# Two weight chunks share runs of equal matmuls

## The chip, the cores and the metric

The kernel runs on one core of one Trainium2 chip. The metric is the device time of one execution in microseconds (us): 1226.41 us is the median of three runs of the kernel before (1226.11 to 1227.22). The engines are TensorE (PE in the rows; PEld are its weight loads), VectorE (DVE), ScalarE (ACT), GpSimd (POOL) and SyncE (SP), whose queue issues nearly all DMAs.

## The reference, cut to what matters

Two transformer blocks run one after the other on 256 tokens of 1024 features, all in float32. Every projection is a product of activations with a large weight matrix that is read from HBM once.

```
x = x + 0.5 * swiglu(rmsnorm(x), ff1_w_gate, ff1_w_up, ff1_w_down)      # d_ff 2816
h = rmsnorm(x); proj = h @ w_in                                         # gMLP, q, k, v, gates
y_a = gmlp_spatial_gating(...); y_b = stick_breaking_attention(q, k, v)
x = x + (g_a * (y_a @ w_branch_a) + g_b * (y_b @ w_branch_b)) @ w_out
x = rmsnorm(x + 0.5 * swiglu(rmsnorm(x), ff2_w_gate, ff2_w_up, ff2_w_down))
# second block, two layers:
for layer in (moba attention, forgetting attention):
    x = x + attention(...) @ w_o[layer]
    x = x + square(relu(rmsnorm(x) @ w_up[layer])) @ w_down[layer]      # 4096 wide
out = rmsnorm(x)
```

## The kernel before, in words

A float32 product is computed with three fp32r products. Each operand is split in a part hi (rounded to fp32r) and a part lo (the rest), and hi * hi + hi * lo + lo * hi is kept.

Weights stream through in **chunks** of 128 x 1024 numbers (512 KB). For every chunk the sync queue fills one of six `raw` buffers; the Scalar engine copies it to one of five `whi` buffers (line 143, `split_hi`); the Vector engine subtracts to make one of four `wlo` buffers (line 150, `split_lo`), and behind each subtraction the DMA of a further chunk is issued. These copies run ahead in program order: before unit u the kernel places the hi copy of chunk u + 3 and the lo copy of chunk u + 2.

A **group** is a set of output columns, mostly 512, that accumulates over its chunks in four PSUM banks; groups alternate between the rings psA and psB of four banks each. A **unit** is the work of PE on one chunk, or on two at the end of some groups. In a *wide* group (all the feed-forward and down projections and some others) the output is transposed: the weights are the stationary operand, and the activations, hi beside lo, move through. A chunk of a group of 512 columns has 128 x 128 weights eight times (two tiles of the inner dimension by four banks). For each there is one **hi matmul** (whi against 512 columns, activations hi and lo) and one **lo matmul** (wlo against 256 columns, activations hi). Line 161 issues all of them.

What sets the order on PE is `unit_mm`. A unit of a wide group does its eight hi matmuls and then its eight lo ones if it is an even unit of the group, and lo first if it is odd. Two chunks in turn are thus hi, lo, lo, hi, and where a pair meets the next one two hi runs join. All engines run the order that the program writes (`manual_schedule`); nothing is reordered later.

The evacuations of a group are queued around the units that follow it: `pre` before the copies of a unit, `mid` between these copies and PE's work, `at` behind it. In a feed-forward part (`ffn`: 11 groups of 4 chunks, each 256 gate and 256 up columns) the Scalar engine copies the upper halves of two banks (line 355), the Vector engine adds the lower halves (361) and multiplies by the norm's factor (563), a Silu follows (566), then the same for the up banks (361, 576), the product (577) and the split of the hidden tile (541, 538). In a squared-ReLU part (`mlp`: 8 groups of 4 chunks) the chain is lines 355, 361, 1055, 1058, 541, 538, once for each half. The norm's factor is computed while the first group of a part (`lead`) is on PE, so the lead's evacuations wait for it and are queued later than those of other groups. A down projection (`down`) has two groups of 512 columns, of 11, 16 or 4 chunks; the last two chunks of its second group share a unit in which bank after bank is finished (`stagger`). `down` is used for the ends of both `ffn`, for the first `mlp`'s end and for w_out, whose input, the merged branches, the Vector and Scalar engines make just ahead of it (lines 937 to 946).

Of the kernel before, what the change touches and what calls it, by code (L numbers as in the profile page):

```python
# [26 lines left out]
class Group:  # L27
# [3 lines left out]


    def __init__(self, ring, srcs, ktiles, xin, tok=False, stagger=0, wide=False, head=0):
        self.head = head
        self.ring, self.srcs, self.ktiles, self.xin = ring, srcs, ktiles, xin
        self.tok, self.stagger, self.wide = tok, stagger, wide
        self.width = sum(c for _, _, c in srcs)
        self.banks = self.width // (128 if wide else 256)
        self.kph = 1024 // self.width
        self.ps = None  # L40
# [3 lines left out]
def decoder_kernel(  # L44
# [58 lines left out]
    def add(g):  # L103
        g.u0 = len(units)
        hs = []
        for k0 in range(0, g.ktiles, g.kph):
            hs.append(len(halves))
            halves.append((g, k0))
        n = len(hs) - g.stagger
        if g.head:  # L110
            units.append((g, hs[:g.head]))
        units.extend((g, [h]) for h in hs[g.head:n])
        if g.stagger:
            units.append((g, hs[n:]))
        g.u1 = len(units) - 1
        return g
# [36 lines left out]
    def unit_mm(u):  # L153
        g, hs = units[u]
        if g.ps is None:
            g.ps = [bank(g.ring) for _ in range(g.banks)]
            g.started = [False] * g.banks
        seq = [(h, kl) for h in hs for kl in range(g.kph)]

        def mm(b, dst, lhsT, rhs, stop):  # L160
            PE.matmul(dst, lhsT, rhs, start=not g.started[b], stop=stop, skip_group_check=True)  # L161
            g.started[b] = True

        def orders(i):

            return (("hi", "lo") if i % 2 == 0 or u < 4 else ("lo", "hi")) if g.wide else ((0, 1, 2),)

        def ws(h, kl, b, parts=(0, 1, 2), end=True):
            k = halves[h][1] + kl
            last = end and k == g.ktiles - 1  # L170
            if g.wide:
                col = kl * g.width + b * 128
                wh, wl = hi_t[h][:, col:col + 128], lo_t[h][:, col:col + 128]
                x = g.xin(k, b)
                if parts == "hi":
                    mm(b, g.ps[b], wh, both(x), last)
                elif parts == "lo":
                    mm(b, g.ps[b][:, :T], wl, x[:, 0, :], last)
                for i in parts if len(parts) == 1 else ():
                    mm(b, g.ps[b][:, T:] if i == 1 else g.ps[b][:, :T], wl if i == 2 else wh,  # L180
                       x[:, int(i == 1), :], False)
                return
            for j in range(2):
                nt = 2 * b + j
                col = kl * g.width + nt * 128
                wh, wl = hi_t[h][:, col:col + 128], lo_t[h][:, col:col + 128]
                x = g.xin(k, nt)
                dst = g.ps[b][:, j * T:(j + 1) * T]
                for i in parts:
                    mm(b, dst, wl if i == 2 else wh, x[:, int(i == 1), :], last and j == 1 and i == 2)  # L190

        def tsm(h, kl, tok, chs, c=slice(0, 512), d=0):
            k = halves[h][1] + kl
            last = k == g.ktiles - 1
            nch = g.width // 512
            xh, xl = (g.xin(k, 0)[:, i, tok * 128:(tok + 1) * 128] for i in range(2))
            for w in (hi_t[h], lo_t[h]):
                for ch in chs:
                    col = kl * g.width + ch * 512
                    b = tok * nch + ch + d  # L200
                    mm(b, g.ps[b][:, :c.stop - c.start], xh, w[:, col + c.start:col + c.stop], False)
            for ch in chs:
                col = kl * g.width + ch * 512
                b = tok * nch + ch + d
                mm(b, g.ps[b][:, :c.stop - c.start], xl, hi_t[h][:, col + c.start:col + c.stop], last)

        if g.tok:
            nch = g.width // 512
            if len(hs) > 1:
                for b in range(g.banks):  # L210
                    n = 1 if b < g.banks - 1 else 2
                    for i in range(n):
                        if i:
                            g.ps.append(bank(flip(g.ring)))
                            g.started.append(False)
                        for h, kl in seq:
                            tsm(h, kl, b // nch, (b % nch,), slice(i * 512 // n, (i + 1) * 512 // n), i)
            else:
                for h, kl in seq:
                    for tok in range(2):  # L220
                        tsm(h, kl, tok, range(nch))
        elif len(hs) > 1:
            for b in range(g.banks):
                o = orders(u - g.u0 + b)
                for i in o:
                    for h, kl in seq:
                        ws(h, kl, b, i, i == o[-1])
        elif u == 0:
            for b in range(g.banks):
                if b == 2:  # L230
                    x_bank(1)
                for i in range(3):
                    for h, kl in seq:
                        ws(h, kl, b, (i,))
        else:
            o = orders(u - g.u0)
            for i in o:
                if u == 1 and i == o[-1]:
                    x_turn(3)
                for h, kl in seq:  # L240
                    for b in range(g.banks):
                        ws(h, kl, b, i, i == o[-1])
# [301 lines left out]
    def ffn(ring, name, wg, wu, wd, slots):  # L544
        r, lead = ring, None
        for i in range(DFF // 256):
            g = add(Group(r, [(wg, 256 * i, 256), (wu, 256 * i, 256)], 8, hn_in, wide=True))
            if lead is None:
                lead = g
                at(g.u0, hidden(name, slots))  # L550
                norm_at(g.u0, r, own=True)

            def gate2(g=g):
                g.gate = second(g, 0, "gt")

            def early(g=g):
                first(g, 0, g.gate)
                first(g, 1, g.up)

            def gate1(g=g):  # L560
                if g is not lead:
                    first(g, 0, g.gate)
                V.tensor_mul(g.gate, g.gate, bc2(R["bc"]))

            def gate0(g=g):
                S.activation(g.gate, g.gate, AF.Silu)
                if g is not lead:
                    g.up = second(g, 1, "ut")

            def up2(g=g):  # L570
                g.up = second(g, 1, "ut")

            def up1(g=g):
                if g is not lead:
                    first(g, 1, g.up)
                V.tensor_mul(g.up, g.up, bc2(R["bc"]))
                V.tensor_mul(g.up, g.up, g.gate)

            def up0(g=g, i=i):
                put_hidden(g.ev + 2, name, 2 * i, g.up)  # L580

            g.ev = max(g.u1, lead.u0 + 5)
            if g is lead:
                at(g.u0 + 4 - (g.u0 > 0), gate2)
                at(g.u0 + 4, up2)
                pre(g.u0 + 5, early)
            else:
                at(g.ev, gate2)
            pre(g.ev + 1, gate1)
            mid(g.ev + 1, gate0)  # L590
            pre(g.ev + 2, up1)
            mid(g.ev + 2, up0)
            r = flip(r)
        return down(r, wd, DFF // 128, fixed_in(name))

    def down(r, w, ktiles, xin, stagger=2):

        return [add(Group((r, flip(r))[i], [(w, 512 * i, 512)], ktiles, xin, stagger=i * stagger, wide=True))
                for i in range(2)]

    at(10, w_s_prep, B)
    for i in range(3):
# [33 lines left out]
    gates = []  # L636
    for i in range(4):
        gates.append(add(Group(r, [(win, 5120 + i * 512, 512)], 8, hn_in, wide=True)))
        r = flip(r)
    norm_at(gates[0].u0, gates[0].ring, cols=True, own=True)  # L640
    lnp = {}
# [37 lines left out]
    for i in range(2):  # L679
        r = flip(r)  # L680
        gu.append(add(Group(r, [(win, 512 * i, 512)], 8, hn_in, wide=True)))

    def gv_evac(b):
        if b == 0:
# [357 lines left out]
    def mlp(ring, name, w, slots):  # L1042
        r, lead = ring, None
        for i in range(8):
            g = add(Group(r, [(w, 512 * i, 512)], 8, hn_in, wide=True))
            if i == 0:
                at(g.u0, hidden(name, slots))
                norm_at(g.u0, r, own=True)
# [345 lines left out]
```

## Time and profile before

| what | value |
|---|---|
| median of three runs | 1226.41 us (1226.11 to 1227.22) |
| profiled execution | 1225.88 us |
| its span | 1224.1 us |
| PE busy | 1214.8 us, 99% of the span |
| weight loads (PEld) busy | 1086.3 us, 89% |
| DVE busy | 893.0 us, 73% |
| ACT busy | 724.0 us, 59% |
| DMA | 219.56 MB, mean 179 GB/s |
| granted TensorE clock | full in all 40 slices |

The span is the time from the first to the last instruction of the program; the execution's own time is 1.8 us longer. Times in rows are us from the span's start. A matmul's duration in a row overlaps the next matmul, so its pace is read from starts. In a timeline, matmuls of one line, tile and shape that follow each other are one row with their count; a window that begins inside a run shows only the rest of the run. Tile names stand without numbers; `hn` is the normed activation, `ffa`, `ffb` and `ma` hidden tiles, `mg` the merged branches, `gt`, `ut` and `rl` temporaries of the evacuations.

### The profile page before, as it was taken

The numbers are of one execution on the slowest core, as the hardware profiler recorded it, in microseconds if no ns is written. First come the engines' busy times: TensorE is split into PE (matmuls) and PEld (weight loads), VectorE is DVE, ScalarE is ACT, GpSimd is POOL, SyncE is SP. The second block draws the span as 40 slices with busy tenths as digits, with TensorE's granted clock in tenths as the row PEclk, the third lists the DMA queues.
The fourth block names the chain that finished last, engine by engine and source line by source line (L and its number), as shares of the span: only waits on it lengthen the run. The fifth ranks groups of instructions, "written<-read, shape, count | busy, mean of one in ns | idle before, by whom it ended". The sixth has DMA issues, their size and how long they took to land.

```text
span 1224.1 us, 20196 instructions
## 1 busy us (share of the span) xinstructions
PE 1214.8 (99%) x7754; PEld 1086.3 (89%) x7754; DVE 893.0 (73%) x1453; ACT 724.0 (59%) x1193; POOL 1.9 (0%) x7
## 2 busy tenths in 40 slices
PE   9999999999999999999999999999999999999997
PEld 8888888889999988888899899888889899888886
DVE  7977756769657688778679767876557767887644
ACT  7655546754666566555466656765446566776433
POOL 0000000000000000000000000000000000000000
PEclk9999999999999999999999999999999999999999
DMA  8666656655444566665565445656564634465651
GB/s 274 214 193 200 208 189 190 191 188 165 152 149 136 160 188 186 192 191 184 190 195 155 142 139 169 189 190 214 165 215 140 232 123 154 156 206 189 227 196 42
DMA packets 143409, 219.56 MB, mean 179 GB/s; under 512 B 10088, under 2 KB 81360, under 8 KB 143312
## 3 DMA queue, kind: packets, MB, share of 16 engines
q1 hardware_dynamic: 141568, 213.79, 54.6%
q10 hardware_dynamic: 1744, 4.48, 1.1%
q8 instruction: 61, 1.00, 0.3%
q14 instruction: 36, 0.29, 0.1%
HBM read 217.17 MB, written 1.06 MB: 178 GB/s over the span
## 4 chain that ended last, share of the span: by engine, by line
PE 96%; DVE 3%; issue 0%; ACT 0%; DMA 0%; DVEq 0%; ACTq 0%
PE psA L161 52%; PE psB L161 37%; PE psB L846 1%; PE psB L825 1%; DVE wlo L150 1%; PE psA L846 1%; PE psA L825 1%; PE psB L888 0%; PE psB L731 0%; DMA xin<-in_x_dram 0%; DVE gv L721 0%; PE psB L890 0%; DVE gv L717 0%; DVE st L706 0%; PE psA L969 0%
## 5 line engine op out<-in xcount | busy, mean ns | idle before, releaser
L150 DVE TENSOR_TENSOR wlo<-raw,whi 128x1024 fp32r<-128x1024 f32 x403 | 483.9, 1219 | 103.8 <-issue 60.5
L143 ACT ACTIVATE whi<-raw 128x1024 fp32r<-128x1024 f32 x403 | 416.4, 1053 | 136.9 <-PE psA L161 81.0
L161 PE MATMUL psA<-hn,whi 128*128 128x512 f32 (+1 forms) x1224 | 267.3, 345 | 0.2 <-ACT whi L1282 0.2
L161 PEld LDWEIGHTS psA<-hn,whi 128*128 128x128 f32 x1224 | 209.6, 190 | 25.9 <-ACT whi L1282 0.4
L161 PE MATMUL psB<-hn,whi 128*128 128x512 f32 (+1 forms) x832 | 196.7, 375 | 0.0
L161 PEld LDWEIGHTS psB<-hn,whi 128*128 128x128 f32 x832 | 149.2, 189 | 25.2
L161 PE MATMUL psA<-hn,wlo 128*128 128x256 f32 x960 | 165.6, 283 | 0.1
L161 PEld LDWEIGHTS psA<-hn,wlo 128*128 128x128 f32 x960 | 139.7, 191 | 4.2 <-DVE wlo L150 0.5
L161 PE MATMUL psB<-hn,wlo 128*128 128x256 f32 x768 | 109.6, 283 | 0.0
L161 PEld LDWEIGHTS psB<-hn,wlo 128*128 128x128 f32 x768 | 102.6, 191 | 3.6
L161 PE MATMUL psA<-whi,mb 128*128 128x512 f32 (+1 forms) x256 | 69.1, 386 | 0.0
L161 PEld LDWEIGHTS psA<-whi,mb 128*128 128x128 f32 x256 | 47.8, 188 | 9.6
L988 ACT ACTIVATE sc<-sc,mx 128x256 f32<-128x256 f32 x64 | 28.4, 445 | 30.7 <-DVE sm L985 30.7
L161 PE MATMUL psA<-whi,hn 128*128 128x512 f32 x128 | 41.7, 395 | 0.0
L161 PE MATMUL psA<-wlo,mb 128*128 128x512 f32 (+1 forms) x128 | 40.3, 386 | 0.0
L161 PE MATMUL psA<-ma,whi 128*128 128x512 f32 x128 | 30.9, 391 | 0.0
L1058 ACT ACTIVATE rl<-rl 128x512 f32<-128x512 f32 x32 | 20.3, 633 | 17.8 <-DVE rl L1055 17.7
L161 PE MATMUL psB<-ma,whi 128*128 128x512 f32 x128 | 30.7, 391 | 0.0
L161 PEld LDWEIGHTS psA<-whi,hn 128*128 128x128 f32 x128 | 24.0, 188 | 5.2
L161 PEld LDWEIGHTS psA<-wlo,mb 128*128 128x128 f32 x128 | 24.0, 188 | 4.9
L386 DVE SCALAR_TENSOR_TENSOR xT<-rs,xT 128x512 f32<-128x512 f32 x16 | 11.0, 688 | 23.7 <-ACT rs L355 23.6
L161 PEld LDWEIGHTS psB<-ma,whi 128*128 128x128 f32 x128 | 23.5, 188 | 4.6
(318 smaller groups left out, 1834.2 us busy)
## 6 DMA issues: line engine op xcount, KB each, us to landing
raw<-in_w_up_dram SPq DMA_DIRECT2D x64, 512.0 KB, 3.9
raw<-in_w_down_dram SPq DMA_DIRECT2D x64, 512.0 KB, 4.0
raw<-in_ff_w_gate_dram SPq DMA_DIRECT2D x88, 256.0 KB, 3.0
raw<-in_ff_w_down_dram SPq DMA_DIRECT2D x44, 512.0 KB, 3.8
raw<-in_ff_w_up_dram SPq DMA_DIRECT2D x86, 256.0 KB, 5.3
raw<-in_w_in_dram SPq DMA_DIRECT2D x40, 512.0 KB, 4.4
raw<-in_w_in_dram SPq DMA_DIRECT2D x32, 256.0 KB, 2.9
raw<-in_moba_w_qkv_dram SPq DMA_DIRECT2D x32, 256.0 KB, 3.9
```

Source lines behind the costliest of these rows:

```text
L143: S.activation(hi_t[h], raw_t[h].rearrange("p k c -> p (k c)"), AF.Copy)
L150: V.tensor_sub(lo_t[h], raw_t.pop(h).rearrange("p k c -> p (k c)"), raw32(hi_t[h]))
L161: PE.matmul(dst, lhsT, rhs, start=not g.started[b], stop=stop, skip_group_check=True)
L386: V.scalar_tensor_tensor(xb, t, alpha, xb, op0=OP.mult, op1=OP.add)
L825: PE.matmul(hb[t][64 * h:64 * h + 64, 384:512], vv[:, k, c:c + 64], w[:, h * 384 + c0:h * 384 + c0 + 128], start=k == 0, stop=k == t, skip ...
L846: PE.matmul(banks[h][:, c:c + n], left[i][rw, cl:cl + 128], right[j][rw, cr:cr + n], start=start and i + j == 0, stop=i == 1, skip_group_c ...
L988: S.activation(s[:, a:b], s[:, a:b], AF.Exp, bias=mx[:, i:i + 1], accum_out=sm[:, i:i + 1])
L1058: S.activation(t, t, AF.Square)
```

## The change

Groups get a flag `pairs`. It is set in all groups of `down`, and in the groups of `ffn` and `mlp` from the third on. In such a group, units are taken two by two, as long as both are single chunks. The first unit of a pair does one kind of matmul for both chunks c and d, the second the other kind, with the chunks in reverse. Even pairs of a group are hi c, hi d, lo d, lo c; odd pairs are lo c, lo d, hi d, hi c. The number of matmuls, the copies and their places in the other engines' queues, the buffers and the units where evacuations are queued stay as they are. A chunk that has no partner and the staggered units keep the old order.

```diff
-            o = orders(u - g.u0)
+            i = u - g.u0
+            singles = g.u1 - g.u0 + (len(units[g.u1][1]) == 1)
+            if g.pairs and i < singles - singles % 2:
+
+                a = u - i % 2
+                hs2 = [units[a][1][0], units[a + 1][1][0]]
+                o = orders(i // 2)
+                for h in hs2 if i % 2 == 0 else hs2[::-1]:
+                    for kl in range(g.kph):
+                        for b in range(g.banks):
+                            ws(h, kl, b, o[i % 2], i % 2 == 1 and h == hs2[1])
+                return
+            o = orders(i)
...
# in ffn and in mlp:
+            g.pairs = i > 1
...
# in down:
+        for g in gs:
+            g.pairs = True
```

The flag is off in groups that the diff doesn't name. There are 96 pairs, 46 of them odd. In PE's whole order a lo matmul of 256 columns is followed by a hi matmul of 512 in 143 places before and in 96 now; the other way round it is 136 and 90.

The first place is PE in the third group of the first feed-forward part (psA; it is the first one with the flag) and the group after it (psB). In the order before:

```order
L161 MATMUL psA<-hn,whi 128x512 x8
L161 MATMUL psA<-hn,wlo 128x256 x16
L161 MATMUL psA<-hn,whi 128x512 x16
L161 MATMUL psA<-hn,wlo 128x256 x8
L329 MATMUL psB<-ident,w_s 128x128 x4
L1341 MATMUL psB<-ident,gains 128x128
L161 MATMUL psA<-hn,wlo 128x256 x8
L161 MATMUL psA<-hn,whi 128x512 x8
L161 MATMUL psB<-hn,whi 128x512 x8
```

And now:

```order
L161 MATMUL psA<-hn,whi 128x512 x16
L161 MATMUL psA<-hn,wlo 128x256 x32
L341 MATMUL psB<-ident,w_s 128x128 x4
L1360 MATMUL psB<-ident,gains 128x128
L161 MATMUL psA<-hn,whi 128x512 x16
L161 MATMUL psB<-hn,whi 128x512 x16
```

The hi matmuls of the third chunk stood ahead of its lo matmuls; now the lo matmuls of the third and fourth chunks follow directly on those of the second and first, and the hi matmuls of both stand behind them.

The second place is PE in the first group of w_out (psB, input mg). Before:

```order
L161 MATMUL psB<-mg_4536,whi 128x512 x8
L161 MATMUL psB<-mg_4536,wlo 128x256 x16
L161 MATMUL psB<-mg_4536,whi 128x512 x8
L161 MATMUL psB<-mg_4537,whi 128x512 x8
L161 MATMUL psB<-mg_4537,wlo 128x256 x16
L161 MATMUL psB<-mg_4537,whi 128x512 x8
```

And now, with the first pair of the second group (psA) behind it:

```order
L161 MATMUL psB<-mg_4536,whi 128x512 x16
L161 MATMUL psB<-mg_4536,wlo 128x256 x16
L161 MATMUL psB<-mg_4537,wlo 128x256 x16
L161 MATMUL psB<-mg_4537,whi 128x512 x16
L161 MATMUL psA<-mg_4536,whi 128x512 x16
L161 MATMUL psA<-mg_4536,wlo 128x256 x16
```

The second pair, on the second half of mg, begins with its sixteen lo matmuls where eight hi matmuls stood ahead of them. The rows of the Vector, Scalar and sync queues are the same in both programs, but for line numbers.

## Rows read from the trace of the kernel before

**Rows 1.** The page's span and its busy times by engine.

```profile
span 1224.1 us, 20196 instructions
PE 1214.8 (99%) x7754; PEld 1086.3 (89%) x7754; DVE 893.0 (73%) x1453; ACT 724.0 (59%) x1193; POOL 1.9 (0%) x7
```

**Rows 2.** PE's waits: who waited for whom, total, times, longest, us.

```profile
PE psB L161 <- DVE wlo L150: 0.9, 2, 0.7
```

**Rows 3.** Timeline of PE in ff1's down projection: start, length, instructions, count.

```profile
135.52 3.82 PE L161 MATMUL psB<-ffa,whi 128*128 128x512 f32 x16
139.18 2.08 PE L161 MATMUL psB<-ffa,wlo 128*128 128x256 f32 x16
141.09 3.82 PE L161 MATMUL psB<-ffa,whi 128*128 128x512 f32 x16
...
157.79 0.40 PE L161 MATMUL psB<-ffa,whi 128*128 128x512 f32 x1
```

**Rows 4.** Timeline of PE, late parts of a hi and a lo run.

```profile
136.91 2.43 PE L161 MATMUL psB<-ffa,whi 128*128 128x512 f32 x10
...
139.77 1.48 PE L161 MATMUL psB<-ffa,wlo 128*128 128x256 f32 x11
```

**Rows 5.** Timelines of PE and DVE: second pairs of three groups, fourth chunk's lo.

```profile
81.70 1.98 PE L161 MATMUL psA<-hn,whi 128*128 128x512 f32 x8
80.72 1.22 DVE L150 TENSOR_TENSOR wlo<-raw,whi 128x1024 fp32r<-128x1024 f32 x1
...
805.90 1.98 PE L161 MATMUL psA<-hn,whi 128*128 128x512 f32 x8
805.11 1.22 DVE L150 TENSOR_TENSOR wlo<-raw,whi 128x1024 fp32r<-128x1024 f32 x1
...
48.30 1.98 PE L161 MATMUL psB<-hn,whi 128*128 128x512 f32 x8
48.18 1.22 DVE L150 TENSOR_TENSOR wlo<-raw,whi 128x1024 fp32r<-128x1024 f32 x1
```

**Rows 6.** Timeline of PE, starts of five second pairs.

```profile
36.62 1.98 PE L161 MATMUL psA<-hn,whi 128*128 128x512 f32 x8
...
430.76 1.98 PE L161 MATMUL psB<-mg,whi 128*128 128x512 f32 x8
...
475.58 1.98 PE L161 MATMUL psB<-hn,whi 128*128 128x512 f32 x8
...
772.38 1.98 PE L161 MATMUL psB<-hn,whi 128*128 128x512 f32 x8
...
1067.34 1.98 PE L161 MATMUL psA<-hn,whi 128*128 128x512 f32 x8
```

**Rows 7.** Timeline of DVE, lo of the fourth chunk in the last four.

```profile
431.61 1.22 DVE L150 TENSOR_TENSOR wlo<-raw,whi 128x1024 fp32r<-128x1024 f32 x1
...
476.44 1.22 DVE L150 TENSOR_TENSOR wlo<-raw,whi 128x1024 fp32r<-128x1024 f32 x1
...
773.89 1.22 DVE L150 TENSOR_TENSOR wlo<-raw,whi 128x1024 fp32r<-128x1024 f32 x1
...
1068.86 1.22 DVE L150 TENSOR_TENSOR wlo<-raw,whi 128x1024 fp32r<-128x1024 f32 x1
```

**Rows 8.** Timeline of DVE in ff1's third group, up to the fourth chunk's lo.

```profile
35.87 0.75 DVE L361 TENSOR_TENSOR ut<-psB,ut 128x256 f32<-128x256 f32 x2
36.65 0.69 DVE L576 TENSOR_TENSOR ut<-ut,rstd 128x512 f32<-128x512 f32 x1
37.38 0.69 DVE L577 TENSOR_TENSOR ut<-ut,gt 128x512 f32<-128x512 f32 x1
37.99 1.22 DVE L150 TENSOR_TENSOR wlo<-raw,whi 128x1024 fp32r<-128x1024 f32 x1
```

**Rows 9.** Timelines of DVE and PE, one handover in the second layer's keys.

```profile
950.24 1.21 DVE L150 TENSOR_TENSOR wlo<-raw,whi 128x1024 fp32r<-128x1024 f32 x1
951.50 0.50 PE L161 MATMUL psB<-wlo,kv 128*128 128x512 f32 x1 [0.23 <-DVE wlo L150]
```

More of the change, by code (lines that the diff above doesn't have):

```diff
@@ L33, in __init__ @@
     def __init__(self, ring, srcs, ktiles, xin, tok=False, stagger=0, wide=False, head=0):
-        self.head = head
+        self.head, self.pairs = head, False
         self.ring, self.srcs, self.ktiles, self.xin = ring, srcs, ktiles, xin
@@ L596, in down @@
     def down(r, w, ktiles, xin, stagger=2):
-        return [add(Group((r, flip(r))[i], [(w, 512 * i, 512)], ktiles, xin, stagger=i * stagger, wide=True))
-                for i in range(2)]
+        gs = [add(Group((r, flip(r))[i], [(w, 512 * i, 512)], ktiles, xin, stagger=i * stagger, wide=True))
+              for i in range(2)]
+        for g in gs:
+            g.pairs = True
+        return gs
     at(10, w_s_prep, B)
@@ L638, in decoder_kernel @@
         gates.append(add(Group(r, [(win, 5120 + i * 512, 512)], 8, hn_in, wide=True)))
+        gates[-1].pairs = False
         r = flip(r)
@@ L681, in decoder_kernel @@
         gu.append(add(Group(r, [(win, 512 * i, 512)], 8, hn_in, wide=True)))
+        gu[-1].pairs = False
     def gv_evac(b):
@@ L1045, in mlp @@
             g = add(Group(r, [(w, 512 * i, 512)], 8, hn_in, wide=True))
+            g.pairs = i > 1
             if i == 0:
```

## The prediction

> **What bounds the kernel now.** I read the busy times first [rows 1]: TensorE (PE) is busy 1214.8 of the 1224.1 us of the span, in 7754 matmuls. So an edit pays only if it makes PE's instructions closer together, and costs whatever it makes PE wait. Next the list of what PE waited for [rows 2]: one entry there concerns a weight copy after the start of the kernel, 0.9 us in all. PE therefore almost never waits, and a wait that the change creates has nothing to hide behind. Durations of matmuls overlap, so I don't use them; I use starts. In a down projection, where nothing else is in PE's queue, runs of 16 hi and 16 lo matmuls alternate [rows 3]. Four whole rounds take 157.79 - 135.52 = 22.27 us, 5.5675 us a round. Late in a run the spacing is even [rows 4]: ten hi matmuls from 136.91 to the lo run's start at 139.18 are 0.227 us apart (2.27 / 10), and eleven lo ones from 139.77 to 141.09 are 0.120 us apart. Sixteen of each at these spacings would take 16 x 0.2267 + 16 x 0.120 = 5.547 us. A round so costs 0.0205 us more than its matmuls: the price of one lo-to-hi border and one hi-to-lo border together.
>
> **What the change removes.** No matmul, no weight copy, no DMA. In PE's whole order the borders at which a 512-column hi matmul follows a 256-column lo one go from 143 to 96, 47 fewer, and those the other way from 136 to 90. Gain: 47 x 0.0205 = 0.96 us, all on PE's path. Bounds: nothing (if a longer run pays the same at its start and again further in), and twice that (if the first matmuls of a run after a long run are cheaper too). I take 0.96, since the hi run's tail in [rows 4] is even up to its end, and a longer run only adds more of the tail.
>
> For this gain the Trainium skill has another answer. "TensorE: Matmul & The Clock Gate", section "Back-to-back issue gap", gives the gap as columns / 2.4 plus 2.5 ns, with no term for the neighbour; by it a border is free, and the gain is nothing, so that the sum would be the stalls alone. The trace disagrees in both points: 227 ns where that page of the Trainium skill has 216 for 512 columns, and 0.0205 us a round for the borders [rows 3, 4].
>
> **What the change moves.** The Vector, Scalar and sync queues keep their order, instruction for instruction; only PE's order changes. So the question is when PE now asks for each weight copy. Call P the start of a pair of chunks c, d on PE. Eight hi matmuls take 1.81 us (8 x 0.227), eight lo ones 0.96.
> - Even pairs. Before: hi c, lo c, lo d, hi d, so that PE wants lo c at P + 1.81 and lo d at P + 2.77. After: hi c, hi d, lo d, lo c, wanting lo d at P + 3.63 and lo c at P + 4.59. All lo demands come later, and hi d is wanted at P + 1.81 instead of 3.73. The hi copies run a chunk further ahead than the lo ones, and their line, 143, stands in no wait of PE; I cost this at nothing. Without that lead it would cost up to 1.92 us a pair.
> - Odd pairs. Before: again hi c, lo c, lo d, hi d, with lo d wanted at P + 2.77. After: lo c, lo d, hi d, hi c: lo c is wanted at P, lo d at P + 0.96. Both demands come 1.81 us earlier, and the Vector engine, which makes lo at 1.22 us a copy between its evacuations, isn't asked any sooner.
>
> So each of the 46 odd pairs must be read: does lo d end before P + 0.96? In a regular feed-forward group it does, narrowly [rows 5]: P = 81.70, demand 82.66, copy 80.72 + 1.22 = 81.94, margin 0.72 us. In a regular group of the squared-ReLU part: 805.90 + 0.96 = 806.86 against 805.11 + 1.22 = 806.33, margin 0.53. There are 16 groups of the first sort and 10 of the second; no stall is forecast in them. Odd pairs in the down projections are as good or better but for one.
>
> Five places fail. They are the first group of each feed-forward part with the new order, where the Vector engine still carries the late evacuations of the group in which the norm was finished, and the first half of the attention block's output projection, where the same engine makes the merged branches. P from [rows 6], copies from [rows 7] and for the first place from [rows 8]:
> - first feed-forward, third group: P = 36.62, demand 37.58; copy 37.99 + 1.22 = 39.21. Late 1.63.
> - output projection: 430.76, demand 431.72; copy ends 432.83. Late 1.11.
> - second feed-forward, third group: 475.58, demand 476.54; copy ends 477.66. Late 1.12.
> - first squared-ReLU part, third group: 772.38, demand 773.34; copy ends 775.11. Late 1.77.
> - second one: 1067.34, demand 1068.30; copy ends 1070.08. Late 1.78.
>
> Can the Vector engine be earlier there? At the first place its rows stand back to back [rows 8]: 35.87, 36.65, 37.38, 37.99, each starting as the one ahead ends, and none waits for PE or for a free buffer, so the new PE order gives it nothing. To each wait belongs the handover from the Vector engine to PE: a lo copy of 950.24 + 1.21 = 951.45 starts its matmul, which was waiting, at 951.50 [rows 9], 0.05 us. Sum: 1.63 + 1.11 + 1.12 + 1.77 + 1.78 + 5 x 0.05 = 7.66 us.
>
> Behind the waiting matmul PE's whole queue stands still, the rest of the group and then all that follows. Could a stall be paid back later? Only where PE waits now and would then arrive late enough not to; that is 0.9 us in all [rows 2]. One pair looks like a sixth place: in the fourth group of the first feed-forward part P = 48.30, demand 49.26, copy 48.18 + 1.22 = 49.40 [rows 5], late by 0.14. I cost it at nothing, since the stall in the group ahead moves P by 1.7 us, while the Vector engine uses that time to work off its backlog.
>
> Buffers: lo c is now held to the end of an even pair and hi c to the end of an odd one, so copies into these buffers can start up to 2.8 us later than now; in the down projections the lo copies then come in bunches of four, and with them the DMAs that refill the raw buffers. Counted in runs of 1.81 and 0.96 us, the next demand for such a lo buffer lies 10 us behind its release, and the lo made out of such a hi buffer is wanted 6.5 us behind it, against 1.22 us for a lo copy and about as much for the hi copy ahead of it. I cost this at nothing; without that cover it would show first as a wait for hi at a group's end.
>
> **Sum.** 7.66 - 0.96 = +6.7 us. The profiled execution took 1225.88 us (span 1224.1 and 1.8 around it), giving 1232.6; it lies 0.5 below the median of the runs, 1226.41, so the forecast on that scale is 1233.1 us, 0.55% slower.
>
> **Rivals.**
> - Not slower: the lo copies arrive in time after all and only the borders count. It decides at P + 0.96 in the five places: were the copies there 1.1 to 1.8 us earlier, nothing is lost, and the time is 1226.4 - 0.96 = 1225.4. For it speaks that margins in all other odd pairs hold; against it, that the queues on the Vector and Scalar engines haven't changed. Chance 0.07.
> - Regular groups stall too: if the later release of a hi buffer pushes the Scalar engine, and it the Vector engine, by 1 us in every group, margins of 0.72 and 0.53 are overrun by 0.28 and 0.47: 16 x 0.28 + 10 x 0.47 = 9.2 us more, 1242. For it: the margins are thin. Against: the Scalar engine's copy at a group's end stands ahead of work that waits for the Vector engine anyway. Chance 0.08.
> - Part of the stalls: only the two largest, 2 x 1.83 - 0.96 = +2.7, 1229.1, if the other three chains shorten. Chance 0.07.
> - Borders free: the stalls of the forecast without a gain, 7.66, 1234.1. This is what the gap by columns alone would make of it. Chance 0.10. It is the rule of the Trainium skill's page that is named above; the border cost in [rows 3, 4] speaks against it.
> - The forecast: 0.68; its own range is 1232.0 to 1234.5 (payback of 0.9 at the low end, no gain and some tenths at the sixth place at the high end).
>
> The range 1229 to 1236 leaves out the first two rivals, 0.15. A measurement of this kernel can tell about 0.2% (2.5 us) from no change: slower 0.88, within 0.2% 0.10 (the first rival and a share of the third), faster 0.02.
>
> **What would show it.** In PE's waits a new entry "PE L161 <- DVE wlo" of five waits, 7.5 us or so, the largest near 1.8; in the timeline the 16-matmul hi runs of the down projections a round of two pairs 11.11 us long instead of 11.135. A sixth wait, or waits spread over all groups, is the second rival; no wait in these five places, with Vector's copies ending at the times of now, would mean that I misread PE's new order, and with copies ending earlier that the chain in [rows 8] was not the engine's own.

## The result, and the profile after

The changed kernel takes 1233.3 us (median of six runs, 1233.1 to 1233.76) against 1226.34 us for the kernel before in the same comparison (six runs, 1225.71 to 1227.33). The ratio is 1.0057, 95% interval 1.0047 to 1.0067: 0.57% slower, where 1233.1 us was forecast. The profiled execution took 1233.4 us.

First the page's span and busy times, which answer to [rows 1].

```profile
span 1231.6 us, 20197 instructions
PE 1215.0 (99%) x7754; PEld 1086.7 (88%) x7754; DVE 893.6 (73%) x1453; ACT 724.6 (59%) x1193; POOL 1.9 (0%) x7
```

The span grew by 7.5 us, while no engine's busy time grew by more than 0.6. Work was not added; it was spread out. PE's list of waits says where, beside [rows 2].

```profile
PE psB L161 <- DVE wlo L150: 3.4, 3, 1.7
PE psA L161 <- DVE wlo L150: 3.2, 2, 1.7
...
PE psB L161 <- ACT whi L143: 1.1, 1, 1.1
```

One of the three in the first row is the wait of 0.7 us that [rows 2] had too. The other five are new, and the timeline of PE places them. Each pair of rows below is the run of lo matmuls of an odd pair: first the 24 that don't wait (sixteen of the even pair, eight of chunk c), then the eight of chunk d.

```profile
35.29 3.03 PE L161 MATMUL psA<-hn,wlo 128*128 128x256 f32 x24
39.86 1.22 PE L161 MATMUL psA<-hn,wlo 128*128 128x256 f32 x8 [1.54 <-DVE wlo L150]
...
431.00 3.03 PE L161 MATMUL psB<-mg,wlo 128*128 128x256 f32 x24
435.14 1.19 PE L161 MATMUL psB<-mg,wlo 128*128 128x256 f32 x8 [1.11 <-ACT whi L143]
...
477.13 3.03 PE L161 MATMUL psB<-hn,wlo 128*128 128x256 f32 x24
481.20 1.22 PE L161 MATMUL psB<-hn,wlo 128*128 128x256 f32 x8 [1.04 <-DVE wlo L150]
482.25 2.91 PE L161 MATMUL psB<-hn,whi 128*128 128x512 f32 x12
...
774.99 3.03 PE L161 MATMUL psB<-hn,wlo 128*128 128x256 f32 x24
779.71 1.22 PE L161 MATMUL psB<-hn,wlo 128*128 128x256 f32 x8 [1.69 <-DVE wlo L150]
...
1071.22 3.03 PE L161 MATMUL psA<-hn,wlo 128*128 128x256 f32 x24
1075.94 1.22 PE L161 MATMUL psA<-hn,wlo 128*128 128x256 f32 x8 [1.70 <-DVE wlo L150]
```

At 0.120 us each, 24 lo matmuls last 2.88 us, so the first place lost 39.86 - 35.29 - 2.88 = 1.69 us, and the others 1.26, 1.19, 1.84 and 1.84: 7.82 in all. The idle times in the brackets are smaller, since they begin at the modelled end of a matmul, not where the next one would have started. Behind a wait the eight matmuls take 482.25 - 481.20 = 1.05 us instead of 0.96; these 0.09 belong to the wait as well (0.07 at w_out).

The Vector engine's lo copies that PE waited for answer to [rows 7, 8]; in the row of 433.78 the copy that PE waits for is the first of three.

```profile
37.97 0.69 DVE L590 TENSOR_TENSOR ut<-ut,gt 128x512 f32<-128x512 f32 x1
38.58 1.22 DVE L150 TENSOR_TENSOR wlo<-raw,whi 128x1024 fp32r<-128x1024 f32 x1
...
433.78 3.49 DVE L150 TENSOR_TENSOR wlo<-raw,whi 128x1024 fp32r<-128x1024 f32 x3
...
479.92 1.22 DVE L150 TENSOR_TENSOR wlo<-raw,whi 128x1024 fp32r<-128x1024 f32 x1
...
778.44 1.22 DVE L150 TENSOR_TENSOR wlo<-raw,whi 128x1024 fp32r<-128x1024 f32 x1
...
1074.67 1.22 DVE L150 TENSOR_TENSOR wlo<-raw,whi 128x1024 fp32r<-128x1024 f32 x1
```

The two rows of the first place are the last two of [rows 8], 0.6 us later, and back to back as there. That offset is older than the first pair: PE's first matmul of the third group starts at 31.66 in this execution and at 31.05 in the other. So the pairs didn't make it; without it the two spans are 6.9 us apart, and the medians are 7.0 apart. Behind every copy PE starts 0.05 to 0.06 us after its end (38.58 + 1.22 = 39.80, 39.86), but at w_out 0.14 (435.00, 435.14).

### The profile page after: what moved, and what is told of

It reads as the page before. It is cut to its first block, busy times and chain, and to the rows that moved or that the text cites. A ratio compares the mean times of both kernels' runs of the same rounds, so it can differ in the third digit from the quotient of the medians.

```text
span 1231.6 us, 20197 instructions
## 1 busy us (share of the span) xinstructions
PE 1215.0 (99%) x7754; PEld 1086.7 (88%) x7754; DVE 893.6 (73%) x1453; ACT 724.6 (59%) x1193; POOL 1.9 (0%) x7
## 3 DMA queue, kind: packets, MB, share of 16 engines
HBM read 217.17 MB, written 1.06 MB: 177 GB/s over the span
## 4 chain that ended last, share of the span: by engine, by line
PE 89%; DVE 7%; DMA 1%; ACT 1%; issue 1%; SPq 0%; DVEq 0%; ACTq 0%
PE psA L161 50%; PE psB L161 34%; DVE wlo L150 2%; PE psB L864 1%; PE psB L843 1%; DMA raw<-in_ff_w_gate_dram 1%; DVE rstd L463 1%; PE psA L864 1%; PE psA L843 1%; PE psB L906 0%; DVE rl L1074 0%; DVE rl L373 0%; PE psB L749 0%; ACT whi L143 0%; DVE gv L739 0%
## 5 line engine op out<-in xcount | busy, mean ns | idle before, releaser
L161 PE MATMUL psA<-hn,whi 128*128 128x512 f32 (+1 forms) x1224 | 264.6, 345 | 0.6 <-DVE hn L1323 0.4
L161 PE MATMUL psB<-hn,whi 128*128 128x512 f32 (+1 forms) x832 | 193.8, 374 | 0.0
L161 PEld LDWEIGHTS psA<-ma,whi 128*128 128x128 f32 x128 | 23.6, 188 | 4.6
```

## The experiments

Every kernel was compared with runs of the kernel before on the same chip; a ratio is to these. The theory: PE waits at the five places because an odd pair asks for lo d 1.81 us sooner and the Vector engine has no slack there; the borders pay 0.96 us back. The rivals: the changed order stalls PE in other ways too, the borders are free, or the lateness is one of buffers or of the Scalar engine.

**New order off at the five places.**

```diff
# in ffn and in mlp:
-            g.pairs = i > 1
+            g.pairs = i > 2
...
     wout = down(SP, w_out[0], 8, fixed_in("mg"))
+    wout[0].pairs = False
```

> The flag is taken from the five places alone: the third groups of both feed-forward and both squared-ReLU parts and the first group of w_out; all other pairs stay. Theory (borders cost 0.0205 us a round, and the whole loss is five waits for a lo copy): the five waits of 1.2 to 1.85 us go, 102 lo-to-hi borders are left against 143 before, 41 x 0.0205 = 0.84 us gained; the sixth place, the fourth group of the first feed-forward part, isn't covered any more and waits 0.14 + 0.05 us. 1226.3 - 0.84 + 0.2 = 1225.7 us. Rival (borders are free): 1226.5. Rival (the loss is spread over all pairs, by buffers held longer): 43 of 48 parts of the loss stay, 1232.5.

Measured: 1225.42 us (11 runs, 1224.91 to 1225.86); ratio 0.9992, 0.9983 to 1.0. The five waits are gone, and of PE's two waits for lo copies before, the one of 0.7 us remains in the list. The timeline of PE in the fourth group of the first feed-forward part shows what is left over there:

```profile
46.68 4.30 PE L161 MATMUL psB<-hn,wlo 128*128 128x256 f32 x32
50.81 3.82 PE L161 MATMUL psB<-hn,whi 128*128 128x512 f32 x16
```

The 32 lo matmuls take 50.81 - 46.68 = 4.13 us instead of 3.84. This is the prediction's sixth place, and with no stall in the group ahead it does stall, by 0.3. The time is what the rival "not slower" would have given, 1225.4, but the interval reaches 1.0, so that a gain over the kernel before isn't shown by it. The five groups make the difference to 1233.3.

**New order at the five places only.**

```diff
# in ffn and in mlp:
-            g.pairs = i > 1
+            g.pairs = i == 2
...
# in down:
-        for g in gs:
-            g.pairs = True
+        gs[0].pairs = ktiles == 8
```

> The complement: pairs in the five places alone, no others (137 lo-to-hi borders). Theory: all five waits, 1.70 + 1.27 + 1.20 + 1.85 + 1.85 = 7.87 us, and 6 x 0.0205 = 0.12 us gained: 1226.3 + 7.75 = 1234.1 us, slower than the change itself. Rival (spread over all pairs): a tenth of the loss, 1227.0.

Measured: 1234.22 us (4 runs); ratio 1.0066, 1.0052 to 1.008. PE's waits:

```profile
PE psB L161 <- DVE wlo L150: 3.7, 4, 1.7
PE psA L161 <- DVE wlo L150: 3.2, 2, 1.7
```

These five groups alone carry the whole loss, 1234.22 with 137 borders beside 1233.3 with 96; the other 86 pairs carry none. With the run before, the rival "regular groups stall too" is out.

**All pairs with hi first.**

```diff
-                o = orders(i // 2)
+                o = orders(0)
```

> All 96 pairs are kept, but every pair is hi c, hi d, lo d, lo c; none begins with lo. Theory: no lo copy is wanted earlier than before the change, so none of the five waits; the borders are 143 lo-to-hi, as many as before, so no gain: 1226.3 us, within 0.3 of before. Rival (pairs as such cost, since two chunks' buffers are held together): the loss stays, 1232 to 1234.

Measured: 1226.05 us (11 runs); ratio 0.9997, 0.9988 to 1.0006. Of PE's waits for lo copies only the old one of 0.7 us is there. The pairs are still there, and each still holds the lo buffer of chunk c to its end; the lo-first order of the second pairs is gone, and with it the loss and the gain of 47 borders. So it is the earlier demand, not the later release of lo buffers, that costs.

**The price of a border.** Here the kernel before does hi first in every unit, with 264 borders where it had 143.

```diff
-            return (("hi", "lo") if i % 2 == 0 or u < 4 else ("lo", "hi")) if g.wide else ((0, 1, 2),)
+            return ("hi", "lo") if g.wide else ((0, 1, 2),)
```

> The kernel before with hi before lo in every unit of a wide group, so that runs never join: 264 lo-to-hi borders instead of 143, and no lo copy is wanted earlier. Theory (0.0205 us a round): 121 x 0.0205 = 2.5 us slower, 1228.8 us, no new wait. Rival (borders are free, as the gap by columns alone has it): 1226.3 us.

Measured: 1227.89 us (11 runs); ratio 1.0015, 1.0006 to 1.0024. The median is 1.5 above before and the span 2.0, where 2.5 was expected. The timeline of PE in the first down projection has the price alone:

```profile
135.15 2.00 PE L161 MATMUL psB<-ffa,whi 128*128 128x512 f32 x8
...
157.50 2.00 PE L161 MATMUL psB<-ffa,whi 128*128 128x512 f32 x8
```

Eight rounds of 8 + 8 take 22.35 us, 2.794 each; at the late spacings of [rows 4] 8 x 0.2267 + 8 x 0.120 = 2.774. A pair of borders costs 0.020 us in short runs as in long ones. The spacings aren't even needed: the same 64 hi and 64 lo matmuls took 22.27 us with four pairs of borders [rows 3] and take 22.35 with eight, 0.02 for each of the four more. Of the 0.5 us that the span lacks, 0.26 is a shorter wait of PE at the keys of the second layer, which is there without more borders too (see the payback below); the rest lies inside the interval.

**Vector engine slowed, in the new order and in the old.** Two products whose results nothing uses are added to the evacuation of each feed-forward group from the fourth on. They run while the group behind it is on PE, ahead of the lo copy of that group's fourth chunk, which had a margin of 0.7 us.

```diff
                 V.tensor_mul(g.up, g.up, g.gate)
+                if i > 2:
+                    for _ in range(2):
+                        V.tensor_mul(g.gate, g.up, g.gate)
```

> The change with two more products of 128 x 512 on the Vector engine ahead of the fourth chunk's lo copy in the eight feed-forward groups from the fourth on, twice (results unused). Each takes 0.69 us, so the copy comes 1.38 us later. Theory (margin of 0.69 us in the profile after, behind it everything is lost): 16 x (1.38 - 0.69 + 0.05) = 11.8 us on top of 1233.3, 1245 us, with 16 new waits of some 0.7 us. Rival (the five waits have another cause than late lo copies, and Vector work under 90% is hidden): 1233 to 1234.

> The same two products per group in the kernel before. Theory: there the fourth chunk's lo copy has a margin of 2.5 us in these groups, 1.38 later costs nothing: 1226.3 us, no new wait. Rival (Vector time is on the path in both kernels): 1238 us, as much slower as with the change.

Measured: 1247.58 us (4 runs), ratio 1.0176, 1.0161 to 1.0191, in the new order; 1225.73 us (10 runs), ratio 0.9998, 0.9988 to 1.0007, in the old one. Rows of one group in the new order, PE and then the Vector engine:

```profile
95.69 3.03 PE L161 MATMUL psB<-hn,wlo 128*128 128x256 f32 x24
99.37 1.21 PE L161 MATMUL psB<-hn,wlo 128*128 128x256 f32 x8 [0.65 <-DVE wlo L150]
```

```profile
96.77 1.42 DVE L593 TENSOR_TENSOR gt<-ut,gt 128x512 f32<-128x512 f32 x2
98.10 1.22 DVE L150 TENSOR_TENSOR wlo<-raw,whi 128x1024 fp32r<-128x1024 f32 x1
```

Each of 16 groups (in both feed-forward parts the fifth to the eleventh, and the first group of the down projection behind them) now loses 99.37 - 95.69 - 2.88 = 0.80 and 0.09 behind it: 16 x 0.89 = 14.2, against 1247.58 - 1233.3 = 14.3. Expected were 0.74 a group; the 0.09 were left out. The same 1.4 us of Vector work is free in the old order and costs 0.9 a group in the new one. That is the cause produced at will, in places where it wasn't: lo d later than demand, and the price is the lateness.

**All lo copies a unit earlier.** If the copies only stood too late in Vector's queue, this should cure the change.

```diff
-LO = 4
+LO = 5
```

> The change with five wlo buffers and every lo copy placed one unit earlier in the Vector queue (before unit u the copy of chunk u + 3, no longer u + 2). Theory (the loss is lo copies that come after a demand moved forward): in the five places the fourth chunk's copy takes the third's slot, in the first one 34.73 to 35.95 against a demand at 37.58, so the five waits vanish and the 0.96 us of borders remain; the waits of 0.4 and 0.9 us in the second layer's keys may go too. 1224.1 to 1225.4 us. Rival (the Vector engine now waits for the Scalar engine's hi copy, made in the same unit, and its evacuations come late): 1227 or more, with waits of PE elsewhere.

> The same five wlo buffers and earlier lo copies in the kernel before, without pairs. Theory: that kernel has no waits in the five places, so only the 1.3 us of waits in the second layer's keys can go: 1225.0 to 1226.4 us, about 1 us above the version with pairs. Rival (earlier lo copies are worth several us by themselves, pairs or not): 1223 or less.

Measured: 1264.33 us (4 runs), ratio 1.0312, 1.0297 to 1.0328, for the changed kernel; 1265.74 us (4 runs), ratio 1.0325, 1.0309 to 1.034, for the kernel before. The five waits went, as expected, but the forecast of the time failed, and the rival was right by more than it said. From the list of PE's waits in the changed kernel:

```profile
PE psA L1021 <- DVE sc L1013: 6.3, 7, 1.9
...
PE psB L455 <- DVE acc L448: 2.2, 1, 2.2
...
PE psA L161 <- DVE wlo L150: 0.8, 1, 0.8
```

One wait for a lo copy is left, at a place that had none before. For the rest, in the attention and norm parts PE now waits for small results of the Vector and Scalar engines that stand behind a copy, and the copy there waits for the Scalar engine's hi copy, as the rival had it. The Vector engine's rows at the norm, ahead of the second wait above:

```profile
656.71 1.23 DVE L150 TENSOR_TENSOR wlo<-raw,whi 128x1024 fp32r<-128x1024 f32 x1 [1.49 <-ACT whi L143]
657.85 0.42 DVE L448 TENSOR_TENSOR acc<-sq,acc 128x256 fp32r<-128x256 f32 x1
```

All waits of the list sum to some 28 us more than before; the span is 37 longer (1261.1), and the granted clock was lower too, 0.995 in the mean against 0.999. The place of a copy is a balance for the whole kernel. The two medians here are 1.4 us apart, but their runs overlap (1263.01 to 1265.27 and 1264.97 to 1266.7) and the clock fell at a place in the one profiled execution where it didn't in the other (see the last section), so that this pair of runs says nothing on the borders.

**Lo copies earlier at four places only.** The lo copy of the fourth chunk directly behind that of the third, with w_out's first group in the old order; in the second version the hi copy too.

```diff
             g.pairs = i > 1
+            if i == 2:
+                ahead.add(g.u0)
...
-            split_lo(units[u][1][-1] + LO - 2)
+            split_lo(units[u][1][-1] + LO - 2 + (u in ahead))
# second version, besides:
-            split_hi(units[u][1][-1] + HI - 2)
+            split_hi(units[u][1][-1] + HI - 2 + (u + 1 in ahead))
```

> The changed kernel, with the new order off in w_out's first group, and with the lo copy of the fourth chunk placed directly behind that of the third in the four other groups that waited, and nowhere else; the hi copies keep their places. My theory: a lo copy can't start before its hi copy ends, and in the changed kernel the fourth chunk's hi copy ends at 36.97 (first feed-forward part), 478.31, 777.90 and 1074.13. A lo copy right behind it ends 1.22 us later: 38.19, 479.53, 779.12, 1075.35, against demands at 38.2, 480.0, 777.9 and 1074.1. So the two feed-forward waits go or shrink below 0.2 us, the two others shrink from 1.85 to about 1.25, and the time is 1233.3 - 1.70 - 1.20 - 1.27 - 2 x 0.6 = 1227.9, some tenths less or more for the waits' second matmuls and one border. Rival: the evacuations that now stand behind the copy come 1.2 to 1.7 us later and cost as much elsewhere as they did where all lo copies were placed a unit ahead: new waits of PE for evacuations or the hidden tile, 1231 or more.

> As e9_lo_ahead_local, and the Scalar engine's hi copy of the fourth chunk is placed behind that of the third too in these four groups. My theory: then the lo copy of the fourth chunk follows that of the third without a wait, ends at about 37.8 (36.55 + 1.22), 477.8 to 479.0, 777.4 and 1073.7, all before the demands at 38.2, 480.0, 777.9 and 1074.1; all five waits are gone and the time is that of the version with the new order off there, less four borders: 1225.3 to 1225.6. Rival: the Scalar engine's extra copy delays the evacuations on which the Vector engine waits, and one or more waits of 0.5 to 1.8 us stay or come up elsewhere: 1227 or more.

Measured: 1227.65 us (11 runs), ratio 1.0011, 1.0002 to 1.002, and 1228.57 us (11 runs), ratio 1.0019, 1.001 to 1.0028. The first number is near the expected 1227.9, but by another way, and the second is a miss. PE in the first version (its lines are one number higher), in the third and fourth groups of the first squared-ReLU part and in the fourth group of the first feed-forward part:

```profile
771.50 4.00 PE L162 MATMUL psB<-hn,wlo 128*128 128x256 f32 x32
...
782.62 3.03 PE L162 MATMUL psA<-hn,wlo 128*128 128x256 f32 x24
786.22 1.22 PE L162 MATMUL psA<-hn,wlo 128*128 128x256 f32 x8 [0.57 <-DVE wlo L151]
...
46.83 3.03 PE L162 MATMUL psB<-hn,wlo 128*128 128x256 f32 x24
50.73 1.22 PE L162 MATMUL psB<-hn,wlo 128*128 128x256 f32 x8 [0.87 <-DVE wlo L151]
```

In the third group the wait is gone altogether (32 in a row): I had taken the hi copy beside the waiting lo copy for the same chunk's; it is the next one's, since hi copies run a chunk further ahead, so the bound in my expectation didn't exist and the second version was needless. But the fourth groups now wait: 1.02, 0.72 and 0.73 us (the last one in the second squared-ReLU part), with 0.09 each 2.7 us. The 1.02 is at the prediction's sixth place, which lost 0.3 with the new order off at the five places. Why the waits moved on, Vector's rows say for the first squared-ReLU part, first of this version and then of the version with the new order off:

```profile
777.22 0.69 DVE L551 TENSOR_TENSOR ma<-rl,ma 128x512 fp32r<-128x512 f32 x1 [1.36 <-ACT ma L554]
...
784.95 1.22 DVE L151 TENSOR_TENSOR wlo<-raw,whi 128x1024 fp32r<-128x1024 f32 x1
```

```profile
775.43 0.69 DVE L550 TENSOR_TENSOR ma<-rl,ma 128x512 fp32r<-128x512 f32 x1 [0.23 <-ACT ma L553]
...
783.15 1.22 DVE L150 TENSOR_TENSOR wlo<-raw,whi 128x1024 fp32r<-128x1024 f32 x1
```

The Vector engine waits there for the Scalar engine's copy of the hidden tile, which waits for the product ahead. The lo copy used to fill that gap; taken out of it, it leaves Vector idle for 1.36 us instead of 0.23, and the backlog that the norm left is worked off one group later. PE's lo run in the fourth group begins 0.85 us later than in the version with the new order off (782.62, there 781.77), the copy for it 1.80 us later. The lateness was passed on, not removed. With the hi copy moved too, PE's idle time at the same place is longer, 0.93 instead of 0.57 us.

No version tried has a lower median than the one with the new order off at the five places, and that one can't be told from the kernel before: its interval ends at 1.0.

## Why the prediction was right

- **Five waits, 7.66 us.** The places, the engine and the sizes were right: forecast with the handover 1.68, 1.16, 1.17, 1.82 and 1.83, measured 1.69, 1.26, 1.19, 1.84 and 1.84. Left out was the second matmul behind each wait, 5 x 0.09. The measured sum is 8.3. At w_out the extra 0.1 is the handover: the profile names the Scalar engine's hi copy as the last releaser, which ended beside the lo copy. Why the matmul should need that one, no run settles.
- **Borders, -0.96 us.** Right in price. In the timeline of PE two pairs in the down projection take 152.61 - 141.50 = 11.11 us, as forecast, against 11.135 in [rows 3]:

```profile
141.50 7.44 PE L161 MATMUL psB<-ffa,whi 128*128 128x512 f32 x32
...
152.61 7.44 PE L161 MATMUL psB<-ffa,whi 128*128 128x512 f32 x32
```

  The run with 264 borders has the same price at half the run length. That was needed: the prediction's spacing of 0.2267 stands in none of its rows, 2.27 / 10 is 0.227, and with it the price would come out at 0.0155. The price sits in the first matmuls of a run, which is why a longer run saves it: in [rows 3, 4] the first six hi matmuls take 136.91 - 135.52 = 1.39 us where six late ones take 1.36, and the first five lo ones 139.77 - 139.18 = 0.59 instead of 0.60. The Trainium skill's "TensorE: Matmul & The Clock Gate", section "Back-to-back issue gap", has no such term; the traces disagree with it, and "borders free" is out. That section gives its formula as the gap of a single matmul by itself, and about 131 ns for 512 columns in a stream, which the prediction left out; the 227 ns here fit neither.
- **Regular margins, 0.72 and 0.53.** Measured in the same two groups 82.10 + 2.88 - 84.28 = 0.70 and 810.28 + 2.88 - 812.65 = 0.51. PE, then the Vector engine:

```profile
82.10 4.00 PE L161 MATMUL psA<-hn,wlo 128*128 128x256 f32 x32
...
810.28 4.00 PE L161 MATMUL psA<-hn,wlo 128*128 128x256 f32 x32
```

```profile
83.06 1.22 DVE L150 TENSOR_TENSOR wlo<-raw,whi 128x1024 fp32r<-128x1024 f32 x1
...
811.43 1.22 DVE L150 TENSOR_TENSOR wlo<-raw,whi 128x1024 fp32r<-128x1024 f32 x1
```

- **The sixth place at nothing,** since the stall ahead moves PE by 1.7 us. Right, and shown both ways: no wait in the changed kernel, and 0.3 us with the new order off at the five places, where the stall ahead is missing.
- **Buffers at nothing.** Right: with the new order off at the five places, the other 86 pairs hold hi and lo buffers as long as forecast, and PE waits for none of them. The lo copies do wait longer for a buffer. In Vector's list of waits, before and then in that run:

```profile
DVE wlo L150 <- PE psB L161: 6.7, 6, 1.5
```

```profile
DVE wlo L150 <- PE psB L161: 29.5, 11, 4.1
```

  The longest such wait is 2.6 us longer, near the 2.8 forecast, and costs PE nothing.
- **Payback up to 0.9.** None is shown. One of the two waits of PE for the keys' lo copies is shorter: from one matmul with wlo to the next it took 951.50 - 950.44 = 1.06 us before and takes 957.36 - 956.55 = 0.81 in the changed kernel. But it is 0.81 too in the old order with the slowed Vector engine, where no stall stands ahead, and 1.07 with the new order at the five places only, where all five stalls are. So it doesn't follow the stalls; what it follows stays open. The other wait, 0.7 us, stayed.

The ledger: 7.82 + 0.45 - 0.96 = +7.3 us, forecast +6.7, measured by the medians +7.0 with an interval from 5.8 to 8.2. The prediction left out the 0.45, which is too little for the medians to show.

## What to carry to other kernels

Where one engine is busy for 99% of the span, a reordering of it is judged by its earliest demands, pair by pair, not by the mean load of the engine that feeds it: one demand 1.8 us earlier costs the lateness and some 0.15 us of starting again, and only where the feeder comes later than the new demand. Here that is where it carries a backlog, behind the norms and the merged branches, and with 1.4 us of added Vector work it is in regular groups too. Keep the old order in the first group or two behind such a backlog. Before a late producer is moved forward, look at what it fills now: work taken out of another engine's wait leaves that wait open, and the lateness comes back one group on.

## What the runs showed of the hardware

Behind a wait the eight lo matmuls took 1.05 us (1.03 at w_out) instead of 0.96. The second of them starts 0.22 us behind the first (0.19 at w_out) instead of 0.12. The weight loads had waited as well: at the first place the first load starts at 39.85 with its matmul at 39.86, where loads otherwise start 0.12 us ahead of theirs (37.92 and 38.04); the second load starts at 39.96 and its matmul again 0.12 behind it. That fits loads that can't run ahead of a wait; no run separates it.

The same idle time left the clock at full in one execution and not in another. With all lo copies a unit earlier, PE waits at the first norm for 1.83 us in the changed kernel and for 1.84 in the kernel before. PE's rows there, of the changed kernel and then of the one before:

```profile
27.00 0.51 PE L455 MATMUL psA<-acc,nones 128*128 128x256 f32 x2 [1.83 <-DVE gt L373]
27.34 2.01 PE L161 MATMUL psB<-hn,whi 128*128 128x512 f32 x8
```

```profile
27.67 0.51 PE L443 MATMUL psA<-acc,nones 128*128 128x256 f32 x2 [1.84 <-DVE gt L361]
28.02 3.19 PE L161 MATMUL psB<-hn,whi 128*128 128x512 f32 x8
```

The eight hi matmuls took 1.85 us from their start to the next run in the one and 2.99 in the other. The granted clock of that stretch (a window of each kernel with its length, busy times with counts, then the clock as a share of full, the DMA share and GB/s; first the changed kernel):

```profile
27.70:31.00 3.30, 3.30 (x24) 2.99 (x23) 3.01 (x3) 3.09 (x4) 0.00 (x0) 1.00 0.99 277
```

```profile
27.70:31.00 3.30, 3.30 (x10) 2.64 (x11) 3.01 (x5) 3.28 (x5) 0.00 (x0) 0.62 0.88 151
```

It was 1.00 in the one and 0.62 in the other, between the levels of 2.4 and 1.2 GHz: the lower level for most of the window. Behind the five waits of the changed kernel the granted clock stayed full, as in all 40 slices of its page. What decides it isn't settled; a wait of this length carries a risk beyond its own price.
